# Order of the u/gate loop of a two-layer decoder trunk: both quarters of a product ahead of the reads of either, and weight sums, splits and loads in another order

## The chip, the cores and the metric

The kernel runs on one core of a Trainium2 chip. The metric is the device time of one launch in microseconds, as the median of three runs. A profile, taken in a separate execution of the same program, gives the span from its first to its last instruction and the times of the single instructions.

## The reference

A prompt of 1024 tokens and 64 sample tokens (8 sequences of 8) with 1024 features pass through two layers, all in fp32. Layer 0 is gated linear attention with four heads. Layer 1, the one that matters here, is a chunked token-mixing MLP, and a final RMSNorm follows:

```python
def cmlp_mixer(h, w_in, ln_g, ln_b, w_spatial, b_spatial, w_out):
    u, v, gate = jnp.split(h @ w_in, 3, axis=-1)
    v = layernorm(v, ln_g, ln_b)
    ...
    mixed = jnp.einsum('gts,bnsgd->bntgd', ws, vg) + bs.T[:, :, None]
    z = u * mixed.reshape(bsz, t, CMLP_WIDTH) * jax.nn.silu(gate)
    return z @ w_out, v
```

Here `h` is the RMS-normalised residual of layer 0's output, `ws` is lower triangular over chunks of 128 tokens, and u, v and gate are each 1024 features wide.

## The kernel before, in words

Features lie on the 128 partitions, in eight blocks, and 1088 token columns (1024 of the prompt, 64 of the sample) on the free axis. To keep fp32 precision each operand is split into a high part (a rounded copy that ScalarE makes) and a low part (the difference, which VectorE makes), and each product is made of three TensorE passes: high by high, high by low, low by high.

The program has five stages: the attention layer; its output projection; the v columns of layer 1 (blocks 16 to 19); the u/gate loop (`for m in range(KT)`, lines 1123 to 1233); and the last output projection with the final norm (`out_proj(28, ...)`). The change is in the u/gate loop and in the last v block, which prepares its first weights.

**The u/gate loop.** A pass m makes 128 features of u and 128 of the gate for all tokens, multiplies them with the mixed v, and stores the result z to DRAM. The product of the [u, gate] weight block (1024 by 256) with the activations is not made directly: it is cut into 2 by 2 blocks in the manner of Strassen and Winograd, which needs seven block products instead of eight. Along the inner dimension the halves are the even and the odd feature blocks, along the outer one u and gate, and the tokens form two halves of 544 columns. Each half is cut into two quarters of 272 columns (`QUART`), since a PSUM bank holds 512 fp32 numbers. So each of the seven products is made for r = 0 and r = 1, 12 matmuls each (`product`, lines 995 to 999). Its weights are four plain blocks, (1,1), (1,2), (2,1), (2,2), of which three are used as they are, and four sums and differences, s1 to s4.

The weights of pass m + 1 are made during pass m. `Quarters(blk)` loads four tiles of 256 KB into the single buffer `rawq` (lines 956 to 960, on SP's queue). `sums` makes s1 to s4 on GpSimd (line 977): s1 first, s2 from s1, s3 by itself, s4 from s2. `parts` and `plain` split a sum or a plain block into its high part on ScalarE (line 964) and its low part on VectorE (line 965); this is called a part below. The buffer `rawq` is free for the next loads when all that reads it is done, the last being the part (1,2).

The results in PSUM: `pb` (tag misc, two buffers) takes the products s2, then s1 and s4 added to it; `pa` (named p1, tag mm) takes (1,1) and later (1,2); `two` is one tile of two banks (tag sc4, one buffer), with quarter r in bank r. It takes s3 first, which ScalarE copies to the gate tile `sg` (line 1145), and later (2,2), which VectorE reads (line 1195). The dependences are tracked for the tile as a whole: where a read of quarter 0 is written ahead of the product for quarter 1, TensorE waits for that read.

Other steps of a pass: ScalarE normalises v (`v_norm`, line 1081, nine chunks of `vm`); GpSimd makes the sample rows of v for output (`v_out`, lines 1089 and 1090, with their gain and bias `bc`) and SP stores them; TensorE mixes v over the tokens (`mixed`, line 1104, and 1098 for the sample), and VectorE writes the result to `zt` (lines 1105 and 1099); GpSimd adds the copied (1,1) product to `p6` (tile half, line 1161) and `sg` (1162); VectorE reads `pb` a last time (1176); GpSimd multiplies it onto `zt` (1177, 1179); then `sg` is multiplied by the tokens' scale `rs`, goes through SiLU on ScalarE (1197) and is multiplied by `rs` again (1206 on GpSimd, 1207 on VectorE); VectorE multiplies `pa` onto `zt` (1210) and `sg` onto `zt` (1211), and SP stores `zt` to `z_d` (1212). `zt`, `sg` and `vm` have one buffer each.

**What sets the order.** From block 16 to the end of the loop the program is under `in_order()`: each engine executes its instructions in the order in which the code writes them. SP's queue, too, issues DMAs in that order, so a DMA that waits holds up all behind it. In pass 0 the four sums of the next block and its parts come at other places than later (`first`); in pass 7 there is no next block, and the loop loads and splits the weights of block 28 and the z of the first token piece instead.

Of the kernel before, what the change touches and what calls it, by code (L numbers as in the profile page):

```python
# [11 lines left out]
ALU = mybir.AluOpType  # L12
# [28 lines left out]
def trunk_kernel(ctx: ExitStack, tc: tile.TileContext, a: dict):  # L41
# [963 lines left out]
    for blk in range(16, 20):  # L1005
        cs = slice((blk - 16) * 256, (blk - 15) * 256)
        for j, i in enumerate((4, 5, 6, 7, 8, 0, 1, 2, 3) if blk == 19 else range(9)):
# [24 lines left out]
            if (blk, j) == (18, 5):  # L1032
                nxt = Quarters(20)
            if blk == 19:
                for f, at in ((t1_load, (1, 2, 5, 6)), (t1_sum, (3, 4, 7, 8)), (t1_split, (5, 6, 8, None))):
                    if j in at:
                        f(at.index(j))
                if j in (1, 2, 3):
                    nxt.sums(("s1", "s2", "s3")[j - 1])
                if j in (3, 4, 5, 6):  # L1040
                    if j == 5:
                        nxt.sums("s4")
                    if j == 6:
                        nxt.plain((1, 1))
                    else:
                        nxt.parts(("s1", "s2", "s3")[j - 3])
                V.bn_aggr(mv[:stats[i].shape[0], i, :], stats[i])
    t1_split(3)
    pr = ps("misc", "pr")
# [73 lines left out]
    for m in range(KT):  # L1123
# [10 lines left out]
        for r in R:  # L1134
            product(pb[r], w["s2"], tq[1][r])
            A.activation(p6[r], pb[r], AF.Copy)
            if first:
                cur.parts("s4") if r == 0 else cur.plain((2, 2))
        V.scalar_tensor_tensor(bias, rsum[:, g, :], lnb[:, m:m + 1], bs[:, g, :], ALU.mult, ALU.add)
        if more and not first:  # L1140
            for key in ("s1", "s2", "s3", "s4"):
                nxt.sums(key, up if key == "s4" else None)
        for r in R:
            product(pe[r], w["s3"], tq[2][r])
            A.activation(sg[:, qb[r]], pe[r], AF.Copy)
            if first and r == 0:
                cur.plain((1, 2))
                nxt = Quarters(21)
        v_norm(vm)
        v_out(m, vm, bc)  # L1150
# [3 lines left out]
        if more and not first:  # L1154
            nxt.parts("s2")
# [9 lines left out]
        V.tensor_tensor(sg[:, fb], sg[:, fb], rs_all[:, fb], ALU.mult)  # L1165
        if more and not first:
            nxt.parts("s3")
            nxt.parts("s1")
        if not more:

            zs = [act_all[:, :, :, lo:lo + n] for lo, n in zip((T - N, 0, N), size)]
            for kt in (0, 2, 4, 6):
                split(zs[0], kt, stage[:, kt, :] if kt < 5 else rest[kt - 5])
        for r in R:
            product(pb[r], w["s4"], b22[r], start=False)
            V.tensor_tensor(p1[r], p1[r], pb[r], ALU.add)
            G.tensor_tensor(zt[:, qb[r]], zt[:, qb[r]], p1[r], ALU.mult) if r == 0 else None
        mixed(zt, vm, g, m, bias, 0, True)
        G.tensor_tensor(zt[:, qb[1]], zt[:, qb[1]], p1[1], ALU.mult)
        if more:  # L1180
            vm = v_load(m + 1)
            if first:
                for key in ("s1", "s2", "s3", "s4"):
                    nxt.sums(key, up if key == "s4" else None)
            else:
                nxt.plain((1, 1))
                nxt.parts("s4")
        else:
            for kt in (1, 3, 5):
                split(zs[0], kt, stage[:, kt, :] if kt < 5 else rest[kt - 5])  # L1190
            load_w(28, 1)
            load_w(28, 2)
        for r in R:
            product(pe[r], w[2, 2], tq[3][r], start=False)
            V.tensor_tensor(sg[:, qa[r]], p6[r], pe[r], ALU.add)  # L1195
        V.tensor_tensor(sg[:, fa], sg[:, fa], rs_all[:, fa], ALU.mult)  # L1196
        A.activation(sg, sg, AF.Silu)  # L1197
        if first:
            for key in ("s2", "s3", "s1"):
                nxt.parts(key)  # L1200
        elif more:
            nxt.plain((2, 2))
        else:
            fetch_w(28, [0, 1])
            load_w(28, 3)
        G.tensor_tensor(sg[:, fb], sg[:, fb], rs_all[:, fb], ALU.mult)
        V.tensor_tensor(sg[:, fa], sg[:, fa], rs_all[:, fa], ALU.mult)
        for r in R:
            product(pa[r], w[1, 2], b21[r], start=False)
            V.tensor_tensor(zt[:, qa[r]], pa[r], zt[:, qa[r]], ALU.mult)  # L1210
        V.tensor_tensor(zt, zt, sg, ALU.mult)
        SP.dma_start(z_d[:, m, :], zt)
        if more:
            if first:
                nxt.plain((1, 1))
                nxt.parts("s4")
                nxt.plain((2, 2))
            nxt.plain((1, 2))
            if m + 2 < KT:
                following = Quarters(22 + m)  # L1220
            else:
                stage = mp.tile([P, 5, N], F32, tag="rawq", name="zstage")
                SP.dma_start(stage, z_d[:, 0:5, 0:N])
                rest = [wp.tile([P, N], F32, tag="raw", bufs=3, name="zmore") for _ in range(2)]
# [3 lines left out]
                following = None  # L1228
            cur, nxt = nxt, following
        else:  # L1230
            for p in range(2):
                split(zs[p], 7, zt[:, N * p:N * p + N])
            fetch_w(28, [2, 3])
# [142 lines left out]
```

## Time and profile before

| what | value |
|---|---|
| three runs | 1013.59, 1009.72, 1012.81 us; median 1012.81 |
| profiled execution, its own time | 1014.11 us |
| its span (first to last instruction) | 1012.3 us |
| mean granted TensorE clock | 0.966 |
| u/gate loop, first matmul of `pb` to first matmul of the last stage | 642.14 to 901.30 us |
| wait of TensorE for the reads of `two` on VectorE (line 1195) | 39.9 us in 8 waits |
| wait of GpSimd's sums for the loads of `rawq` | 65.6 us |

A row of a group says: line, engine, operation, output and inputs by tile name, shape, count; then busy time in all and mean duration of one; then the idle time of the engine just before, and what ended it. PE is TensorE's matmul, PEld its weight load, DVE VectorE, ACT ScalarE, POOL GpSimd, SPq SyncE's issuing of DMAs. A row of a timeline says: start, duration, instruction, count, and in brackets the idle time before it. A row of windows says: the stretch, its length, busy time and count of PE, PEld, DVE, ACT and POOL, then the granted share of TensorE's clock, the DMA engines' busy share, and GB/s. The chain of waits is followed back from the last instruction: at each step to what released it.

### The profile page before, as it was taken

Reading aid. Unit: us, or ns where it says so; the run is one execution under the profiler, and the core shown is the slowest. Engines: PE = TensorE matmul, PEld = TensorE weight load, DVE = VectorE, ACT = ScalarE, POOL = GpSimd, SP = SyncE. Lnnn points to the kernel's source line nnn. Section 1 sums busy time; section 2 is a strip of 40 time slices with the busy share of each in tenths; the row PEclk is TensorE's granted clock in tenths of the full one; section 3 lists DMA queues with packets and bytes.
Section 4 is the critical chain, followed back from the end, with each engine's and each line's share of the span. In section 5 each row is a group of like instructions: output and inputs, shape, how many; then the busy total and the mean of one; then the engine's idle time right before and its main releaser. Section 6 shows DMA issues by size and latency. Waiting matters only on the chain.

```text
span 1012.3 us, 17078 instructions
## 1 busy us (share of the span) xinstructions
PE 927.9 (92%) x6437; PEld 897.3 (89%) x6437; DVE 624.5 (62%) x1279; ACT 461.6 (46%) x972; POOL 283.6 (28%) x315
## 2 busy tenths in 40 slices
PE   8989999999999999899999999888797778879995
PEld 7979899989999999889999998877797778879995
DVE  7797887587758776785357555553444544484245
ACT  8673555255535554642454554633342234345332
POOL 2032242233223322221411002044432544211123
PEclk9999999999999999899999999989988889899998
DMA  8302112221231124246734445411212022355233
GB/s 279 85 3 75 58 58 69 89 58 50 76 89 58 38 84 110 65 126 188 238 99 135 149 134 174 134 52 63 91 67 90 24 90 90 107 189 148 61 102 124
DMA packets 89967, 101.80 MB, mean 101 GB/s; under 512 B 9862, under 2 KB 80844, under 8 KB 89884
## 3 DMA queue, kind: packets, MB, share of 16 engines
q1 hardware_dynamic: 89884, 100.71, 32.0%
q8 instruction: 50, 0.82, 0.3%
q14 instruction: 33, 0.27, 0.1%
HBM read 74.26 MB, written 26.42 MB: 99 GB/s over the span
## 4 chain that ended last, share of the span: by engine, by line
PE 46%; DVE 23%; DMA 9%; POOL 7%; issue 7%; ACT 6%; SPq 1%; DVEq 0%; POOLq 0%; ACTq 0%
PE fm L137 23%; PE tm L151 10%; DVE wq L965 4%; PE two L999 3%; DMA rawq<-w 3%; DMA xsum<-x_spill 2%; POOL qsum L977 2%; DVE act L198 1%; PE sc L513 1%; POOL qs L977 1%; POOL half L1161 1%; POOL sg L1162 1%; PE o L623 1%; DVE scT L526 1%; DMA xt<-x_spill 1%
## 5 line engine op out<-in xcount | busy, mean ns | idle before, releaser
L137 PE MATMUL fm<-act,w 128*128 128x384 f32 (+1 forms) x2208 | 390.6, 333 | 3.7 <-DVE zt L1210 2.5
L137 PEld LDWEIGHTS fm<-act,w 128*128 128x128 f32 x2208 | 367.6, 189 | 7.9 <-issue 2.7
L151 PE MATMUL tm<-w,act 128*128 128x256 f32 (+1 forms) x1536 | 193.5, 283 | 3.2 <-ACT vt L1010 2.2
L151 PEld LDWEIGHTS tm<-w,act 128*128 128x128 f32 x1536 | 185.6, 188 | 5.5 <-ACT vt L1010 3.1
L999 PE MATMUL two<-tsum,wq 128*128 128x272 f32 x384 | 65.8, 329 | 43.8 <-DVE sg L1195 39.9
L999 PEld LDWEIGHTS two<-tsum,wq 128*128 128x128 f32 x384 | 59.5, 223 | 47.3 <-DVE sg L1195 41.6
L123 DVE TENSOR_TENSOR w<-wr,w 128x512 fp32r<-128x512 f32 (+1 forms) x96 | 68.9, 732 | 22.6 <-ACT w L122 21.8
L122 ACT ACTIVATE w<-wr 128x512 fp32r<-128x512 f32 (+1 forms) x96 | 58.5, 624 | 28.5 <-DMA wr<-w 16.2
L821 POOL TENSOR_TENSOR acc<-acc,sq 128x384 f32<-128x384 f32 (+1 forms) x30 | 30.1, 1008 | 111.2 <-ACT sq L816 110.9
L999 PE MATMUL p<-act,wq 128*128 128x272 f32 x384 | 55.1, 303 | 0.0
L843 DVE TENSOR_TENSOR x<-fm,res 128x384 f32<-128x384 f32 (+1 forms) x40 | 20.9, 526 | 54.4 <-PE fm L137 54.4
L999 PEld LDWEIGHTS p<-act,wq 128*128 128x128 f32 x384 | 54.2, 205 | 0.0
L999 PE MATMUL pb<-act,wq 128*128 128x272 f32 x384 | 51.4, 290 | 0.0
L816 ACT ACTIVATE sq<-x 128x384 f32<-128x384 f32 (+1 forms) x42 | 20.9, 503 | 61.8 <-DVE x L843 59.6
L999 PEld LDWEIGHTS pb<-act,wq 128*128 128x128 f32 x384 | 49.0, 189 | 0.0
L1197 ACT ACTIVATE sg<-sg 128x1088 f32<-128x1088 f32 x8 | 8.9, 1114 | 84.8 <-DVE sg L1196 84.8
L468 POOL TENSOR_TENSOR xe<-xe,k 128x384 f32<-128x384 f32 (+2 forms) x24 | 29.1, 1213 | 44.3 <-ACT xe L467 41.1
L654 POOL TENSOR_TENSOR on<-on,g 128x384 f32<-128x384 f32 (+1 forms) x24 | 23.8, 1013 | 57.4 <-DVE on L653 34.7
L977 POOL TENSOR_TENSOR qsum<-rawq 128x512 f32<-128x512 f32 x16 | 20.7, 1296 | 65.7 <-DMA rawq<-w 65.6
L444 POOL TENSOR_TENSOR kd<-kd,k 128x384 f32<-128x384 f32 (+1 forms) x12 | 12.0, 1003 | 84.5 <-ACT kd L443 84.5
L965 DVE TENSOR_TENSOR wq<-qsum,wq 128x512 fp32r<-128x512 f32 x25 | 19.6, 810 | 26.0 <-ACT wq L964 26.0
L475 DVE TENSOR_TENSOR xl<-cum 128x192 f32<-128x192 f32 (+4 forms) x72 | 35.0, 511 | 0.0
(260 smaller groups left out, 1580.6 us busy)
## 6 DMA issues: line engine op xcount, KB each, us to landing
wr<-w SPq DMA_DIRECT2D x92, 256.0 KB, 3.1
rawq<-w SPq DMA_DIRECT2D x32, 256.0 KB, 4.5
xsum<-x_spill SPq DMA_DIRECT2D x16, 272.0 KB, 3.1
z_spill<-zt SPq DMA_DIRECT2D x8, 544.0 KB, 3.0
s<-s SPq DMA_DIRECT2D x16, 256.0 KB, 4.2
state_s<-ns SPq DMA_DIRECT2D x32, 128.0 KB, 1.8
v_spill<-vt SPq DMA_DIRECT2D x32, 128.0 KB, 3.0
vm<-v_spill SPq DMA_DIRECT2D x8, 512.0 KB, 4.2
```

Of the source, the lines that this page charges most:

```text
L122: A.activation(w[:, 0], raw, AF.Copy)
L123: V.tensor_tensor(w[:, 1], raw, w[:, 0].bitcast(F32), ALU.subtract)
L137: PE.matmul(acc, lhs, rhs, start=(k == 0), stop=(k == 23))
L151: PE.matmul(acc, lhs, rhs, start=(k == 0), stop=(k == 23))
L468: G.tensor_tensor(xe, xe, kt_[:, :nl], ALU.mult)
L475: V.tensor_tensor(l3[:, :, lo:hi], c3[:, :, (i + 1) * m:], r, ALU.subtract)
L654: G.tensor_tensor(o, o, gate[h][:, j, t0:t0 + n], ALU.mult)
L816: A.activation(sq, raw[p][:, m, :], AF.Square)
L821: (V if gain is not None and p == 2 or m == KT - 1 else G).tensor_tensor(total, acc[p], sq, ALU.add)
L965: V.tensor_tensor(w[:, 1], src, w[:, 0].bitcast(F32), ALU.subtract)
L977: G.tensor_tensor(t, x, y, op)
L999: PE.matmul(acc, lhs, rhs, start=start and k + i == 0, stop=k + i == 5, skip_group_check=not start)
```

## The change

Three things change, and no arithmetic on TensorE.

First, at both uses of `two` the products of both quarters are now written ahead of the reads of either: s3 ahead of ScalarE's copies, and (2,2) ahead of VectorE's reads.

Second, the preparation of the next weights is in one order for all passes. The sums s1 and s2 stand ahead of GpSimd's adds to `half` and `sg`, s3 behind them, and s4 behind `v_out`, which moves from the normalisation to behind the two products onto `zt`. The parts s2, s3, s1 stand ahead of the reads of `two`, then (1,1), (2,2) and (1,2); s4's part moves to the start of the pass that uses it. The next loads of `rawq` follow the part (1,2) directly, ahead of the reads of `pa` and the store of z, which is now issued behind these loads. Four of the nine normalisations of v move ahead of ScalarE's copies of `two` in passes 1 to 7. The product of `rs` and half of `sg` after SiLU moves from GpSimd to VectorE.

Third, at the edges: the first loads of `rawq` are called two steps later in v block 18, the first sums and parts in block 19 lie one step later, the tile `pr` moves from tag misc to tag o, and in pass 7 weight loads and splits are spread otherwise, with the last product onto `zt` in two pieces.

```diff
-            if (blk, j) == (18, 5):
+            if (blk, j) == (18, 7):
                 nxt = Quarters(20)
...
-    pr = ps("misc", "pr")
+    pr = ps("o", "pr")
...
         for r in R:
             product(pb[r], w["s2"], tq[1][r])
             A.activation(p6[r], pb[r], AF.Copy)
-            if first:
-                cur.parts("s4") if r == 0 else cur.plain((2, 2))
+        cur.parts("s4")
+        if first:
+            for key in ((1, 2), (2, 2)):
+                cur.plain(key)
+            nxt = Quarters(21)
...
-        if more and not first:
-            for key in ("s1", "s2", "s3", "s4"):
-                nxt.sums(key, up if key == "s4" else None)
         for r in R:
             product(pe[r], w["s3"], tq[2][r])
+        if not first:
+            v_norm(vm, range(4))
+        for r in R:
             A.activation(sg[:, qb[r]], pe[r], AF.Copy)
...
-        v_norm(vm)
-        v_out(m, vm, bc)
+        v_norm(vm, range(0 if first else 4, 9))
...
-        if more and not first:
-            nxt.parts("s2")
+        if more:
+            for key in ("s1", "s2"):
+                nxt.sums(key)
...
-        V.tensor_tensor(sg[:, fb], sg[:, fb], rs_all[:, fb], ALU.mult)
-        if more and not first:
-            nxt.parts("s3")
-            nxt.parts("s1")
-        if not more:
+        if more:
+            nxt.sums("s3")
+        else:
...
         G.tensor_tensor(zt[:, qb[1]], zt[:, qb[1]], p1[1], ALU.mult)
+        v_out(m, vm, bc)
         if more:
+            nxt.sums("s4", up)
             vm = v_load(m + 1)
...
+        V.tensor_tensor(sg[:, fb], sg[:, fb], rs_all[:, fb], ALU.mult)
+        if more:
+            for key in ("s2", "s3", "s1"):
+                nxt.parts(key)
...
         for r in R:
             product(pe[r], w[2, 2], tq[3][r], start=False)
+        for r in R:
             V.tensor_tensor(sg[:, qa[r]], p6[r], pe[r], ALU.add)
+        if more:
+            nxt.plain((1, 1))
...
-        G.tensor_tensor(sg[:, fb], sg[:, fb], rs_all[:, fb], ALU.mult)
         V.tensor_tensor(sg[:, fa], sg[:, fa], rs_all[:, fa], ALU.mult)
-        for r in R:
-            product(pa[r], w[1, 2], b21[r], start=False)
-            V.tensor_tensor(zt[:, qa[r]], pa[r], zt[:, qa[r]], ALU.mult)
-        V.tensor_tensor(zt, zt, sg, ALU.mult)
-        SP.dma_start(z_d[:, m, :], zt)
+        V.tensor_tensor(sg[:, fb], sg[:, fb], rs_all[:, fb], ALU.mult)
         if more:
...
             nxt.plain((1, 2))
             if m + 2 < KT:
                 following = Quarters(22 + m)
...
+        for r in R:
+            product(pa[r], w[1, 2], b21[r], start=False)
+            V.tensor_tensor(zt[:, qa[r]], pa[r], zt[:, qa[r]], ALU.mult)
+        for part in ((slice(0, T),) if more else (slice(0, N), slice(N, T))):
+            V.tensor_tensor(zt[:, part], zt[:, part], sg[:, part], ALU.mult)
...
+        SP.dma_start(z_d[:, m, :], zt)
```

Lines of the changed kernel are some three to six lower or higher than before: the reads of `two` are at 1194, the adds to `half` and `sg` at 1158 and 1159, the last product onto `zt` at 1217.

On TensorE, in a later pass (any of 2 to 6), from the sample's mixing to the product (1,2) in `pa`; the tile names are those of the code, `tsum` are the activation's sums, and brackets name the engines whose semaphore a matmul waits for. Before:

```order
L1098 MATMUL mix<-wss,vm 128x64 [waits DVE_49,Activation_49,Pool_49]
L999 MATMUL two<-tsum_6114,wq 128x272 x12
L999 MATMUL two<-tsum_6114,wq 128x272 [waits DVE_49]
L999 MATMUL two<-tsum_6114,wq 128x272 x11
L999 MATMUL p_8380<-act,wq 128x272 [waits Activation_49]
L999 MATMUL p_8380<-act,wq 128x272 x11
```

After:

```order
L1095 MATMUL mix<-wss,vm 128x64 [waits DVE_49,Activation_49,Pool_49]
L999 MATMUL two<-tsum_6114,wq 128x272 x24
L999 MATMUL p_8370<-act,wq 128x272 [waits Activation_49]
L999 MATMUL p_8370<-act,wq 128x272 x11
L999 MATMUL p_8371<-act,wq 128x272 [waits Activation_49]
```

The 24 matmuls of both quarters of (2,2) now follow each other without a wait between them; before, the thirteenth waited for VectorE.

On GpSimd in one such pass (`half` is p6 and the copied (1,1) product, `qsum` are s1, s2, s3 and `qs4` is s4). Before, from the first sum:

```order
L977 TENSOR_TENSOR qsum_8030<-rawq_7986 128x512
L977 TENSOR_TENSOR qsum_8032<-qsum_8030,rawq_7986 128x512
L977 TENSOR_TENSOR qsum_8034<-rawq_7986 128x512
L977 TENSOR_TENSOR qs4_8036<-rawq_7986,qsum_8032 128x512
L1089 TENSOR_TENSOR bc_7994<-vm_7912,bc_7994 64x128
L1090 TENSOR_TENSOR bc_7994<-bc_7994 64x128
L1161 TENSOR_TENSOR half_7999<-half_7999,half_8001 128x272
L1162 TENSOR_TENSOR sg_7993<-sg_7993,half_8001 128x272
L1161 TENSOR_TENSOR half_8000<-half_8000,half_8002 128x272
L1162 TENSOR_TENSOR sg_7993<-sg_7993,half_8002 128x272
L1177 TENSOR_TENSOR zt_7992<-zt_7992,half_8001 128x272
L1179 TENSOR_TENSOR zt_7992<-zt_7992,half_8002 128x272
```

After, from the first sum:

```order
L977 TENSOR_TENSOR qsum_8366<-rawq_8230 128x512
L977 TENSOR_TENSOR qsum_8368<-qsum_8366,rawq_8230 128x512
L1158 TENSOR_TENSOR half_8271<-half_8271,half_8273 128x272
L1159 TENSOR_TENSOR sg_8265<-sg_8265,half_8273 128x272
L1158 TENSOR_TENSOR half_8272<-half_8272,half_8274 128x272
L1159 TENSOR_TENSOR sg_8265<-sg_8265,half_8274 128x272
L977 TENSOR_TENSOR qsum_8414<-rawq_8230 128x512
L1176 TENSOR_TENSOR zt_8264<-zt_8264,half_8273 128x272
L1178 TENSOR_TENSOR zt_8264<-zt_8264,half_8274 128x272
L1086 TENSOR_TENSOR bc_8266<-vm_8177,bc_8266 64x128
L1087 TENSOR_TENSOR bc_8266<-bc_8266 64x128
L977 TENSOR_TENSOR qs4_8450<-rawq_8230,qsum_8368 128x512
```

The four sums and the two operations on `bc` stood ahead of the adds to `half` and `sg`; now two sums do, and s3, `bc` and s4 stand behind.

On VectorE, the end of such a pass (`wq<-qsum` is the part of a sum, `wq<-rawq` of a plain block, `wq<-qs` of s4). Before, from the last reads of `pb`:

```order
L1176 TENSOR_TENSOR half<-half,pb 128x272 x2
L1099 SCALAR_TENSOR_TENSOR zt<-mix,lng,bias 128x64
L965 TENSOR_TENSOR wq<-rawq,wq 128x512
L965 TENSOR_TENSOR wq<-qs_8586,wq 128x512
L1195 TENSOR_TENSOR sg<-half,two 128x272 x2
L1196 TENSOR_TENSOR sg<-sg,rs 128x544
L965 TENSOR_TENSOR wq<-rawq,wq 128x512
L1207 TENSOR_TENSOR sg<-sg,rs 128x544
L1210 TENSOR_TENSOR zt<-p_8655,zt 128x272
L1210 TENSOR_TENSOR zt<-p_8656,zt 128x272
L1211 TENSOR_TENSOR zt<-zt,sg 128x1088
L965 TENSOR_TENSOR wq<-rawq,wq 128x512
```

After, from the parts of the sums, which follow the last reads of `pb`, the sample's mixing and a product with `rs`:

```order
L965 TENSOR_TENSOR wq<-qsum,wq 128x512 x3
L1194 TENSOR_TENSOR sg<-half,two 128x272 x2
L965 TENSOR_TENSOR wq<-rawq,wq 128x512
L1197 TENSOR_TENSOR sg<-sg,rs 128x544
L965 TENSOR_TENSOR wq<-rawq,wq 128x512
L1203 TENSOR_TENSOR sg<-sg,rs 128x544
L1204 TENSOR_TENSOR sg<-sg,rs 128x544
L965 TENSOR_TENSOR wq<-rawq,wq 128x512
L1215 TENSOR_TENSOR zt<-p_8370,zt 128x272
L1215 TENSOR_TENSOR zt<-p_8371,zt 128x272
L1217 TENSOR_TENSOR zt<-zt,sg 128x1088
L965 TENSOR_TENSOR wq<-qs_8450,wq 128x512
```

The last row of `wq<-rawq`, which frees the buffer for the next loads, stood behind the last product onto `zt`; now it stands ahead of the reads of `pa`. The reads of `two` now stand next to each other with one part less ahead of them, and s4's part ends the pass.

On SP's queue the four loads of `rawq` followed the store of z in each pass, and the store now follows them; the loads of the next `vm`, behind the store of the v rows in both, now wait for the later operations on `bc`.

More of the change, by code (lines that the diff above doesn't have):

```diff
@@ L1037, in trunk_kernel @@
                         f(at.index(j))
[L1038 to L1046, printed above, removed]
+                if j in (2, 3, 4, 6):
+                    nxt.sums({2: "s1", 3: "s2", 4: "s3", 6: "s4"}[j])
+                if j in (4, 5, 6):
+                    nxt.parts(("s1", "s2", "s3")[j - 4])
+                if j == 7:
+                    nxt.plain((1, 1))
                 V.bn_aggr(mv[:stats[i].shape[0], i, :], stats[i])
     t1_split(3)
-    pr = ps("misc", "pr")
+    pr = ps("o", "pr")
     PE.matmul(pr, ones, ws.rearrange("p g t -> p (g t)"), start=True, stop=True)
@@ L1176, in trunk_kernel @@
             V.tensor_tensor(p1[r], p1[r], pb[r], ALU.add)
-            G.tensor_tensor(zt[:, qb[r]], zt[:, qb[r]], p1[r], ALU.mult) if r == 0 else None
+            if r == 0:
+                G.tensor_tensor(zt[:, qb[r]], zt[:, qb[r]], p1[r], ALU.mult)
         mixed(zt, vm, g, m, bias, 0, True)
         G.tensor_tensor(zt[:, qb[1]], zt[:, qb[1]], p1[1], ALU.mult)
+        v_out(m, vm, bc)
         if more:
+            nxt.sums("s4", up)
             vm = v_load(m + 1)
[L1182 to L1187, printed above, removed]
+        V.tensor_tensor(sg[:, fb], sg[:, fb], rs_all[:, fb], ALU.mult)
+        if more:
+            for key in ("s2", "s3", "s1"):
+                nxt.parts(key)
         else:
@@ L1190, in trunk_kernel @@
                 split(zs[0], kt, stage[:, kt, :] if kt < 5 else rest[kt - 5])
-            load_w(28, 1)
-            load_w(28, 2)
+            load_w(28, 3)
         for r in R:
             product(pe[r], w[2, 2], tq[3][r], start=False)
+        for r in R:
             V.tensor_tensor(sg[:, qa[r]], p6[r], pe[r], ALU.add)
+        if more:
+            nxt.plain((1, 1))
         V.tensor_tensor(sg[:, fa], sg[:, fa], rs_all[:, fa], ALU.mult)
         A.activation(sg, sg, AF.Silu)
[L1198 to L1201, printed above, removed]
+        if more:
             nxt.plain((2, 2))
         else:
-            fetch_w(28, [0, 1])
-            load_w(28, 3)
-        G.tensor_tensor(sg[:, fb], sg[:, fb], rs_all[:, fb], ALU.mult)
+            fetch_w(28, [1, 2])
         V.tensor_tensor(sg[:, fa], sg[:, fa], rs_all[:, fa], ALU.mult)
-        for r in R:
-            product(pa[r], w[1, 2], b21[r], start=False)
-            V.tensor_tensor(zt[:, qa[r]], pa[r], zt[:, qa[r]], ALU.mult)
-        V.tensor_tensor(zt, zt, sg, ALU.mult)
-        SP.dma_start(z_d[:, m, :], zt)
+        V.tensor_tensor(sg[:, fb], sg[:, fb], rs_all[:, fb], ALU.mult)
         if more:
[L1214 to L1217, printed above, removed]
             nxt.plain((1, 2))
@@ L1223, in trunk_kernel @@
                 SP.dma_start(stage, z_d[:, 0:5, 0:N])
+                following = None
+        for r in R:
[3 more added lines that the diff above has]
+            V.tensor_tensor(zt[:, part], zt[:, part], sg[:, part], ALU.mult)
+            if not more:
+                k = int(part.start > 0)
+                split(zs[k], 7, zt[:, N * k:N * k + N])
+        SP.dma_start(z_d[:, m, :], zt)
+        if more:
+            if m + 2 == KT:
                 rest = [wp.tile([P, N], F32, tag="raw", bufs=3, name="zmore") for _ in range(2)]
@@ L1227, in trunk_kernel @@
                 load_w(28, 0)
[L1228 removed]
             cur, nxt = nxt, following
         else:
[L1231 to L1233 removed]
+            fetch_w(28, [3])
     order.close()
```

6 lines of the change are left out of this document (3 added, 3 removed).

## Prediction

> **What bounds the kernel now.** I read the page first: span and TensorE's share of it.
>
> ```profile
> span 1012.3 us, 17078 instructions
> PE 927.9 (92%) x6437; PEld 897.3 (89%) x6437; DVE 624.5 (62%) x1279; ACT 461.6 (46%) x972; POOL 283.6 (28%) x315
> ```
>
> TensorE is the busy engine, but 92% is a mean over stages. Then the groups by line, for the line that the change is about, and the windows of one pass of the u/gate loop, of a stretch after its long wait, and of the stage behind the loop.
>
> ```profile
> L999 PE MATMUL two<-tsum,wq 128*128 128x272 f32 x384 | 65.8, 329 | 43.8 <-DVE sg L1195 39.9
> 734.90:767.20 32.30, 25.68 (x187) 25.25 (x187) 14.62 (x23) 10.72 (x23) 12.76 (x14) 0.87 0.22 71
> 767.20:770.20 3.00, 3.00 (x13) 3.00 (x14) 0.00 (x0) 0.00 (x0) 0.00 (x0) 0.50 0.00 0
> 910.20:1012.30 102.10, 90.55 (x536) 88.64 (x536) 45.02 (x74) 36.78 (x69) 23.28 (x21) 0.97 0.35 111
> ```
>
> TensorE waits 39.9 us in all for VectorE's reads of the first quarter of `two` (L1195), and after such a wait runs some 3 us at a granted clock of 0.50. What is a pass worth to TensorE alone? The timeline of TensorE in one pass:
>
> ```profile
> 751.35 3.18 PE L999 MATMUL p<-act,wq 128*128 128x272 f32 x24
> 754.37 1.95 PE L1104 MATMUL mix<-ws,vm 128*128 128x128 f32 x16
> 756.07 3.26 PE L999 MATMUL pb<-act,wq 128*128 128x272 f32 x24
> 767.19 1.05 PE L999 MATMUL two<-tsum,wq 128*128 128x272 f32 x3 [6.13 <-DVE sg L1195]
> ```
>
> A pair of quarters takes 3.02 us from start to start (751.35 to 754.37), the mixing 1.70 (754.37 to 756.07). Seven pairs (21.14), the mixing and 0.11 for the sample's mixing (an estimate: eight mixings of 128 columns take 1.70, this one has 64) make 22.95 us. A pass takes 32.3. So 9.3 us of each pass are waits and slow clock, more than the 5 us that the waits for L1195 sum to per pass. Why is VectorE late? The chain of waits through the same pass:
>
> ```profile
> 743.93 1.29 DVE zt L1211
> 745.22 0.60 DVE wq L965
> 746.24 0.72 SPq L959
> ...
> 747.53 4.75 DMA rawq<-w
> ...
> 752.51 1.29 POOL qsum L977
> ...
> 753.88 1.34 POOL qsum L977 x2
> ...
> 756.35 1.75 POOL qs L977
> ...
> 759.00 0.76 POOL half L1161
> ...
> 761.22 0.72 POOL sg L1162
> ...
> 762.61 1.29 DVE wq L965 x2
> 763.89 0.69 DVE half L1176 x2
> ...
> 764.78 2.00 DVE wq L965 x2
> 766.78 0.36 DVE sg L1195
> ...
> 767.19 3.10 PE two L999 x12
> ...
> 770.79 0.74 DVE sg L1196
> ...
> 773.27 1.50 DVE wq L965
> 774.77 0.64 DVE sg L1207
> ...
> 776.21 1.29 DVE zt L1211
> 777.50 0.60 DVE wq L965
> ```
>
> This is a ring, and it sets the period: L1211 starts at 743.93 and 776.21, 32.28 us apart. The one buffer `rawq` is free when VectorE has made the last part of its block (L965 at 745.22); then come the loads, all four sums on GpSimd, the bias rows, the half/sg adds, VectorE's parts and L1195, the second quarter on TensorE, and the tail of the pass down to the next last part. TensorE's long wait is one link of it.
>
> **The change, part by part.** The new ring is put together from the same rows. (a) Loads: the z store is now issued behind them. From the last part's end (745.82) to the first sum (752.51) is 6.69 us today with the store ahead; without it, one issue 0.72, the data 4.75 and 0.22 of hand-over make 5.69. Bounds 5.2 and 6.7; I take 5.7. (b) Only s1 and s2 stand ahead of the half/sg adds: 753.88 less 752.51 is 1.37, and 1.29 more, 2.66; today all four sums and the bias rows stand there (752.51 to 759.00, 6.49). (c) The four adds, 759.00 to 761.94, stay: 2.94. (d) Second read of pb 0.35, sample's mixing 0.20, the product with rs 0.64, together 1.2. (e) Three parts, 1.29 for two, so 1.93. (f) Both reads of `two`, 0.36 each, which now follow each other, 0.72; TensorE's 3.10 between them leaves the ring. (g) Part (1,1) 0.64 and the product with rs 0.74. (h) From that product's end (771.53) over SiLU and ScalarE's copy to the next part (773.27) 1.74. (i) Part (2,2), two products with rs and part (1,2): 2.52. The reads of pa and L1211 (2.09 today, 775.41 to 777.50) leave the ring, since part (1,2) now goes ahead of them. Sum: 5.69 + 2.66 + 2.94 + 1.2 + 1.93 + 0.72 + 1.38 + 1.74 + 2.52 = 20.8.
>
> To this comes what GpSimd and VectorE do to each other. Timelines of both engines:
>
> ```profile
> 740.57 1.37 POOL L1206 TENSOR_TENSOR sg<-sg,rs 128x544 f32<-128x544 f32 x1 [6.37 <-ACT sg L1197]
> 740.98 1.51 DVE L965 TENSOR_TENSOR wq<-rawq,wq 128x512 fp32r<-128x512 f32 x1 [1.76 <-ACT wq L964]
> ```
>
> The part that takes 0.60 alone takes 1.51 beside L1206 and ends 0.55 after it. This meeting goes (L1206 moves to VectorE, +0.64 there, counted in i). But s3, the two zt products, the bias rows and s4 now run on GpSimd just while VectorE makes d, e and g: two sums of 1.29 and four pieces of at most 0.76, 5.6 us in all. The cost is 0 if they never meet, 5.6 if VectorE stands still through all of them. In the row above the part lost 0.91 of the 1.37 it met; at that rate all pieces would cost 3.7. I take that somewhat over half of them are met, 2.15 (0.45 for the product in d, 1.0 for the parts e, 0.7 behind s4). The ring is then 22.95 (20.8 to 26.4).
>
> The Trainium skill (page "SBUF — State Buffer", section "SBUF: two separate sides") has a rule that speaks against this order: a VectorE operation with two SBUF inputs and a GpSimd operation that reads SBUF lock each other out for the whole instruction. By the rule at its worst the ring would be 26.4 and the kernel about 972; without any lock it would be 20.8, and TensorE's 22.95 the bound. The trace agrees that there is a lock (1.51 against 0.60); how often they meet in the new order, no row shows.
>
> So ring and TensorE (both 22.95) are even, and two that are even don't mesh without loss: I forecast 23.4 us a pass, an estimate that allows 0.45 for hand-overs. To the count of passes and the two ends:
>
> ```profile
> L1211 DVE TENSOR_TENSOR zt<-zt,sg x8: 1279/1292/1295, 677.9 to 901.9; 128x1088 f32<-128x1088 f32 x8
> 872.54 1.30 DVE zt L1211
> 873.86 3.13 DMA z_spill<-zt
> ...
> 878.01 4.33 DMA bc<-lnbc
> ...
> 883.45 0.66 POOL half L1161
> 901.30 1.98 PE L137 MATMUL fm<-act,w 128*128 128x384 f32 x10 [2.48 <-DVE zt L1210]
> 646.53 2.45 PE L999 MATMUL pb<-tsum,wq 128*128 128x272 f32 x12 [2.32 <-ACT rsum L1051]
> ```
>
> Six passes from the first L1211 to the seventh take 872.54 - 677.9 = 194.6 us, 32.4 each; at 23.4 they take 140.4, which is 54.2 less. The last pass, from the seventh L1211's end (873.84) to the next stage's first product (901.30), takes 27.46. Of this, 9.6 pass before the half adds (store, 4.33 for the bias rows behind other loads, two small operations). In the new order those adds don't stand behind the bias rows and can start when ScalarE's copy is there, about 3 us in; 6.6 are gained there, and the second quarter's wait goes as well, which I put at 0.9, since the splits of `zmore` behind it still wait for the z store. I take 7.5 less (5 to 9). At the start, `pr` in its own buffer takes away the 2.32 us wait; VectorE's and ScalarE's weights stand right behind it, so I count 1.0 (0 to 2.3). Moving the first block's loads from step 5 to 7 and its sums by one step lies beside the v products on TensorE; I count nothing, and were that cover gone, one load time of 6.7 at the worst. Given back: the last stage was fed by loads that have no more time than before, and its products start 7.5 us nearer to them; 1.5 (0 to 4). Sum: 54.2 + 7.5 + 1.0 - 1.5 = 61.2 us.
>
> The profiled execution took 1014.11 us, 1.8 more than its span; the median of the three runs is 1012.81. 1012.81 - 61.2 = 951.6, rounded to 952.
>
> **The rivals.** (1) A longer ring: the loads stay at 6.7 and VectorE and GpSimd stand in each other's way twice as much (4.3). The ring is then 22.95 + 1.0 + 2.15, and 0.4 for hand-overs, 26.5; the six passes give 35, and the time is about 970. For it: the pieces do lie beside each other. Against: the z store's data no longer stand ahead of the loads. This is the rule of the Trainium skill's page "SBUF — State Buffer" named above, taken near its worst. (2) The z store, now behind 1 MB of loads, holds the single zt buffer: the first mixing result (L1105 before, L1102 now) waits for it, and TensorE's sample product stands behind that. L1217 ends 2.1 after the last part, when 3.4 of the loads' 5.5 us are left, and the store alone takes 3.13: landing at most 6.5 after L1217, the result 0.7 later. TensorE needs the first of the parts e at about 11.5 after L1217 for its next pass and has two pairs (6.04) to do between, so it comes to the sample product at 5.5 or later. The wait is at most 1.7 us a pass; at 1.5 the time is 961. For it: there is one buffer only. Against: the store's data may overlap the loads'. (3) Slower than before: ScalarE now normalises four chunks of v ahead of its copies of `two`, and their load stands in SP's queue behind v_out, which waits for the bias rows, now late on GpSimd.
>
> ```profile
> DMA to landing us min/median/max: 3.7/4.0/4.2
> ```
>
> That is the load of vm. The first sum starts 3.6 after L1217 (5.7 less 2.1); b, c, s3 and 3.5 for the zt and bias pieces bring the issue to 14 and the landing to 18. The four normalisations stand 3 us ahead of the copies of `two`, which wait for the next L1217 at 23.4, so the load is wanted at about 20. Each us beyond that adds up to one to every pass; the kernel is slower than before from a landing some 9 us late, after 29. Nothing in the trace holds this load that long. (4) No change: the ring is tied to something the trace does not show, and keeps 32.3. Against it: links (a), (b) and (f) are explicit in the chain and are cut in the new order.
>
> **How the numbers follow.** My forecast, with (2) as its upper part, 0.80; rival 1, 0.13; rival 4, 0.03; rival 3, 0.04. The forecast's own bounds: TensorE's floor of 22.95 in all passes (57), 9 at the end and 2.3 at the start, nothing given back, make 68 and 944; 24.9 a pass, (2)'s price, make 52 and 961. Rival 1 reaches to 970, a bit of it beyond. So 944 to 972. A measurement of this kernel tells about 0.5% from no change, 5 us: faster by more 0.93, within 0.03, slower 0.04.
>
> **What would show it.** In the changed profile L1217 starts every 23 to 24 us; the group two<-tsum loses its wait for the reads of `two` and its mean comes down from 329 ns towards 290; the granted clock in the loop is above 0.95; the first sum starts 5.5 to 6 us after the last part; the chain of waits in the loop names TensorE's products for a good part. I am wrong if TensorE waits over 2 us a pass anywhere (then by whom: L1102 for rival 2, weights for rival 1, L1145 for rival 3), if the period is over 26, or if the stage behind the loop takes over 115 us against 111.0 today (901.30 to 1012.3).

## The result and the profile after

The changed kernel takes 952.25 us (median of 4 runs, 951.49 to 953.75) beside 1011.26 (4 runs, 1007.81 to 1013.59): 0.942 of the time, with a 95% interval of 0.939 to 0.945. The forecast was 952. The profiled execution took 951.55 with a span of 949.8.

First the page's head and two of TensorE's groups by line (the prediction shows the head and the group `two` of before):

```profile
span 949.8 us, 17088 instructions
PE 909.2 (96%) x6437; PEld 882.1 (93%) x6437; DVE 630.6 (66%) x1288; ACT 458.8 (48%) x972; POOL 279.8 (29%) x307
L999 PE MATMUL pb<-act,wq 128*128 128x272 f32 x384 | 52.1, 292 | 5.3 <-ACT half L1133 5.2
L999 PE MATMUL two<-tsum,wq 128*128 128x272 f32 x384 | 51.6, 290 | 0.0
```

The products into `two` wait for nothing now (43.8 us before) and take 290 ns each (329). What TensorE still waits for in the loop is 5.2 us in all, for ScalarE's copy of pb (L1133). A window of one pass, from 0.33 us behind the end of one L1217 (744.37) to as much behind the end of the next, shows the granted clock (its last columns are clock, share and rate of the DMA engines):

```profile
744.70:768.19 23.49, 23.38 (x188) 23.16 (x188) 15.74 (x25) 10.25 (x24) 12.23 (x13) 1.00 0.30 95
```

TensorE is busy for 23.4 of these 23.5 us at a clock of 1.00 (0.87 in the pass of before). It would be easy to read this as "TensorE sets the pass". The chain of waits from the first sum in this pass to the first sum of the next says otherwise:

```profile
748.13 1.28 POOL qsum L977
...
750.74 0.77 POOL half L1158
...
752.96 0.74 POOL sg L1159
...
754.36 1.15 DVE sg L1183
755.51 0.71 DVE wq L965
...
756.62 2.12 DVE wq L965 x2
758.74 0.69 DVE sg L1194 x2
759.43 1.43 DVE wq L965
760.87 0.65 DVE sg L1197
...
762.55 0.62 ACT wq L964
...
763.20 0.69 DVE wq L965
763.89 0.63 DVE sg L1203
764.53 0.64 DVE sg L1204
765.16 0.61 DVE wq L965
...
767.17 4.66 DMA rawq<-w
...
772.00 1.28 POOL qsum L977
```

There is no product in it. It is the ring through the buffer `rawq`, sum to sum 23.87 us here. The first seven L1217 end at 670.73, 695.27, 719.72, 744.37, 767.86, 791.72 and 816.39: 24.28 a pass on average, against 32.44 before.

Where the 62.5 us between the two profiled spans went, by stage (landmarks: the first `tm` product of the v stage, the first product of the loop, the ends of the first and seventh zt*sg, the first `fm` product, the end):

| stretch | before | after | difference | forecast |
|---|---|---|---|---|
| up to the v stage | 539.15 | 536.49 | -2.7 | 0 |
| v stage | 102.99 | 100.19 | -2.8 | 0 |
| first pass | 37.03 | 34.05 | -3.0 | -1.0 |
| six passes | 194.67 | 145.66 | -49.0 | -54.2 |
| last pass | 27.46 | 20.54 | -6.9 | -7.5 |
| last stage | 111.0 | 112.87 | +1.9 | +1.5 |

The code ahead of the v stage is the same in both kernels; its start lies between 535.3 and 538.2 in the profiles of all the experiments, so the 2.7 there belongs to no edit. The profiled execution of before took 1014.11, longer than the median of 1011.26: so the spans differ by 62.5 and the medians by 59.0.

### The profile page after: what moved, and what is told of

Same layout as the page of the kernel before. It is cut to its first block, busy times and chain, and to the rows that moved or that the text cites. A ratio compares the mean times of both kernels' runs of the same rounds, so it can differ in the third digit from the quotient of the medians.

```text
span 949.8 us, 17088 instructions
## 1 busy us (share of the span) xinstructions
PE 909.2 (96%) x6437; PEld 882.1 (93%) x6437; DVE 630.6 (66%) x1288; ACT 458.8 (48%) x972; POOL 279.8 (29%) x307
## 3 DMA queue, kind: packets, MB, share of 16 engines
q1 hardware_dynamic: 89884, 100.71, 34.1%
## 4 chain that ended last, share of the span: by engine, by line
PE 46%; DVE 24%; DMA 11%; issue 6%; ACT 6%; POOL 5%; SPq 2%; DVEq 0%; POOLq 0%; ACTq 0%
PE fm L137 26%; PE tm L151 10%; DVE wq L965 4%; DMA rawq<-w 3%; DMA xsum<-x_spill 3%; DMA wr<-w 1%; PE sc L513 1%; POOL qsum L977 1%; PE o L623 1%; PE pst L584 1%; SPq L959 1%; POOL half L1158 1%; DVE sg L1183 1%; DMA xt<-x_spill 1%; DVE scT L526 1%
## 5 line engine op out<-in xcount | busy, mean ns | idle before, releaser
L999 PE MATMUL two<-tsum,wq 128*128 128x272 f32 x384 | 51.6, 290 | 0.0
L999 PE MATMUL p<-act,wq 128*128 128x272 f32 x384 | 51.0, 288 | 0.0
L999 PEld LDWEIGHTS p<-act,wq 128*128 128x128 f32 x384 | 49.4, 188 | 0.0
L999 PEld LDWEIGHTS two<-tsum,wq 128*128 128x128 f32 x384 | 49.1, 188 | 0.0
L964 ACT ACTIVATE wq<-qsum 128x512 fp32r<-128x512 f32 x25 | 15.0, 626 | 52.3 <-POOL qsum L977 52.3
L1102 DVE SCALAR_TENSOR_TENSOR zt<-mix,lng,bias 128x512 f32<-128x512 f32 x16 | 11.4, 747 | 31.9 <-DMA z_spill<-zt 21.3
```

Source lines behind the costliest of these rows:

```text
L999: PE.matmul(acc, lhs, rhs, start=start and k + i == 0, stop=k + i == 5, skip_group_check=not start)
```

## The experiments

Two theories were set against each other. **Ring theory** (the prediction's; a ring is a chain of waits that closes on itself from one pass to the next): the loop through the one buffer `rawq` (loads, sums, adds, parts) sets the pass, and the pair edit only takes one link out of it. **Pair theory**: the pair edit removes TensorE's waits and slow clock, 9 us a pass, and the order of sums, parts and loads is worth little. Ratios and differences are to the kernel before on the same chip in the same session (medians 1012.38 for the first four, 1012.23 for the next four, 1011.52 for the last three). "Pass" is the mean of the six passes in the profile.

| kernel | us | ratio, 95% interval | pass |
|---|---|---|---|
| pair edit alone | 984.58 | 0.973 (0.970 to 0.975) | 28.68 |
| order alone (all of the change but the pair edit) | 1000.0 | 0.987 (0.984 to 0.990) | 30.74 |
| loads behind the store | 969.67 | 0.958 (0.955 to 0.961) | 27.14 |
| parts and loads early | 945.84 | 0.935 (0.932 to 0.937) | 22.98 |
| store after the loads | 946.71 | 0.935 (0.932 to 0.938) | 23.45 |
| s1 twice | 962.93 | 0.950 (0.946 to 0.954) | 25.55 |
| early, s1 twice | 946.37 | 0.935 (0.932 to 0.938) | 23.23 |
| edges as before | 954.55 | 0.944 (0.940 to 0.947) | 24.33 |
| rs on GpSimd | 951.4 | 0.939 (0.936 to 0.942) | 24.37 |
| order alone, s1 twice | 999.94 | 0.988 (0.985 to 0.991) | 30.61 |
| early, and late store | 946.27 | 0.935 (0.933 to 0.938) | 23.49 |

**The pair edit alone**, in the kernel before (the same at the second use of `two`):

```diff
         for r in R:
             product(pe[r], w["s3"], tq[2][r])
+        for r in R:
             A.activation(sg[:, qb[r]], pe[r], AF.Copy)
```

> The kernel before, with one edit: at both uses of `two` both quarters' products stand ahead of both reads. Ring theory (the loop through the one buffer rawq sets the pass; the pair edit cuts one link of it): the link is the second quarter's 3.10 us on TensorE and some 0.3 of hand-over, 3.4 a pass; the sums, bias rows and loads stay, so L1211 comes every 28.9 us (32.3 less 3.4), seven passes of gain make 24 and the last 1 to 3: about 985 us (980 to 991). Pair theory (TensorE's waits for the reads of `two` and the half clock behind them, 9.3 us a pass, are the loss, and the pair edit takes them away whatever the order of the weights): a pass of 23.5, about 950 to 958.

It took 984.58 with passes of 28.68, where the ring theory had 985 and 28.9. TensorE no longer waits for the reads of `two`, but for something else; its waits, and two lines of the chain in a pass:

```profile
PE mix L1098 <- DVE zt L1105: 17.7, 5, 4.4
```

```profile
762.98 4.39 DMA rawq<-w
...
774.00 0.75 POOL half L1162
```

The wait has moved to the sample's mixing, where TensorE arrives early and stands behind VectorE's mixing (L1105, at 771.89 in this pass). This stands behind the part of s2, whose high part on ScalarE (L964) waits for GpSimd's sums and so for the loads. VectorE's timeline:

```profile
770.89 1.08 DVE L965 TENSOR_TENSOR wq<-qsum,wq 128x512 fp32r<-128x512 f32 x1 [7.92 <-ACT wq L964]
```

What comes later in the ring waits for GpSimd's adds, and these start 6.6 us after the loads' data (767.37), because all sums and the bias rows stand ahead. As a whole explanation the pair theory falls here.

**The order alone**, the reads put back between the quarters:

```diff
-        for r in R:
-            product(pe[r], w["s3"], tq[2][r])
         if not first:
             v_norm(vm, range(4))
         for r in R:
+            product(pe[r], w["s3"], tq[2][r])
             A.activation(sg[:, qb[r]], pe[r], AF.Copy)
 ...
         for r in R:
             product(pe[r], w[2, 2], tq[3][r], start=False)
-        for r in R:
             V.tensor_tensor(sg[:, qa[r]], p6[r], pe[r], ALU.add)
```

> The kernel after, with the reads of `two` put back between the two quarters at both uses (the first four normalisations then stand ahead of the products); the new order of sums, parts and loads stays. Ring theory: the second quarter's products (3.1) come back into the ring of 24.3, with 0.2 to 0.4 of hand-over: 27.6 a pass, six passes 20 and the last pass 3 more: about 974 (966 to 982). The gains of this kernel (some 38 over the kernel before) and of the pair edit alone (some 27) then add up to that of the whole change (59). Pair theory: the waits of 6 us are back and the order of the weights is worth little: 995 to 1010.

It took 1000.0, which the ring theory missed by 26 and the pair theory had. The chain of waits through a pass shows why:

```profile
770.48 0.29 ACT sg L1144
...
770.82 1.78 PE two L999 x12
772.59 3.00 PE pb L999 x24
775.60 3.03 PE p L999 x24
778.63 1.78 PE mix L1101 x16
780.41 3.02 PE pb L999 x24
...
783.55 0.44 DVE half L1173
...
784.19 0.63 DVE sg L1182
784.82 4.11 DVE wq L965 x3
788.93 0.36 DVE sg L1192
...
789.33 2.39 PE two L999 x12
791.72 3.93 PE p L999 x24
```

This is a second ring that has neither loads nor sums in it. TensorE's products feed VectorE (L1173); behind that stand the product with rs and three parts; the read of the first quarter (L1192) stands behind these; and TensorE's second quarter, and so all its later products, waits 4.18 us for that read and 1.32 for ScalarE's copy. With the slow products after the wait (2.2 a pass: the groups p and two take 57.6 and 62.7 us in all, against 51.0 and 51.6) and TensorE's own 22.95 it makes 30.6. I had counted the interleaving as one link of 3.1 in the first ring; it closes a ring of its own. So the theory is amended: **two rings**, one through `rawq` and one through TensorE and the reads of `two`, and the longer one sets the pass.

**The second ring, put to a test**: s1 made twice in this kernel, which lengthens only the ring through `rawq`.

```diff
-            for key in ("s1", "s2"):
+            for key in ("s1", "s1", "s2"):
                 nxt.sums(key)
```

> The kernel with the new order but the reads of `two` between the quarters (1000.0 us), with the sum s1 made twice. Its chain of waits runs through TensorE, ScalarE and VectorE and not through the loads and sums. If that second ring sets its pass (30.6), the 1.29 more on GpSimd is inside the idle time ahead of the half/sg adds (1.2) and costs 0 to 0.3 a pass: 999 to 1003. If the ring through rawq sets it, 1.29 on each of seven passes: 1009.

999.94 against 1000.0, passes of 30.61: it cost nothing, as the two rings have it. (Before the adds GpSimd stands idle for 1.21 us in a pass of the kernel above, so nearly all of the 1.29 had room there. No run lengthens the second ring by itself: that it sets this pass rests on its chain and on this test.)

**The same dose in the changed kernel** (the same edit):

> The kernel after, with the sum s1 of each block made twice (one more GpSimd operation of 1.29 us ahead of the half/sg adds, with the same result). Ring theory: GpSimd's sums stand in the ring, so each of the seven passes grows by 1.29: 9 us, 961 (959 to 963). If the pass were TensorE's (23.1 of 24.3), no more than a part of it would show: 952 to 955.

962.93: 10.7 more than the changed kernel by the medians of two sessions, 8 by the ratios. In the profile the pass grew by 1.27 to 25.55, which is 7.7 over six passes, and the first pass by 2.1. Although TensorE is busy for 23.4 us of a pass, GpSimd's 1.29 passes straight into the time. In one pass the chain of waits names the z store ahead of s2 (6.14 us, then L1102, which ends at 760.32). But s2 starts at 760.34, 0.08 after the second s1, as it does after s1 in the changed kernel, so the store holds nothing up there.

**Loads behind the store again:**

```diff
-            if m + 2 < KT:
-                following = Quarters(22 + m)
 ...
         SP.dma_start(z_d[:, m, :], zt)
         if more:
+            if m + 2 < KT:
+                following = Quarters(22 + m)
```

> The kernel after, with the next block's loads issued behind the z store again. The store waits for L1217, which ends 2.1 us after the last part, so the loads start 2.1 to 2.5 later. Ring theory: the pass grows by that, less what the loads gain by having fewer of the store's packets at their end (0 to 1): 25.8 to 26.8 a pass, 9 to 15 more over six passes: 961 to 967. Pair theory: TensorE sets the pass and 0.5 to 1.3 a pass is slack: 952 to 955, and no growth of the period beyond 0.5.

969.67, more than the 961 to 967 that I had put down: the loads are issued 0.55 after L1217's end instead of 2.02 ahead of it, 2.57 later, the first sum comes 2.9 later, and the pass takes 2.86 more. The delay goes through one to one; what I had allowed the loads to get back, they didn't get. (In pass 6 the load of z for the next stage, which follows the same lines, moves with them.)

**The store after the loads**, on ScalarE's queue in the next pass (for passes 0 to 5):

```diff
-        zt = up.tile([P, T], F32, tag="zt", name="zt")
 ...
             A.activation(p1[r], pa[r], AF.Copy)
+        if 0 < m < KT - 1:
+            A.dma_start(z_d[:, m - 1, :], zt)
+        zt = up.tile([P, T], F32, tag="zt", name="zt")
 ...
-        SP.dma_start(z_d[:, m, :], zt)
+        if m + 2 >= KT:
+            SP.dma_start(z_d[:, m, :], zt)
```

> The kernel after, with the z store of passes 0 to 5 issued on ScalarE's queue in the next pass, behind the two copies of p1, some 2.7 to 3.3 us after L1217 and so near the end of the rawq loads instead of at their start; zt is allocated again behind it. Theory A (the loads stayed at 6.7 us because the store's packets share the engines with them): without it the first sum comes 1.0 earlier, as step (a) of the forecast had it; the pass falls from 24.3 to 23.3, which is near TensorE's 23.1: 945 to 948. Theory B (the loads take that long by themselves): no gain there, and the first mixing result now waits up to 0.6 longer for zt: 951 to 956.

946.71. The table of DMA issues (the last number is the median us from issue to landing), first of the changed kernel, then of this one:

```profile
rawq<-w SPq DMA_DIRECT2D x32, 256.0 KB, 3.8
...
z_spill<-zt SPq DMA_DIRECT2D x8, 544.0 KB, 6.0
```

```profile
rawq<-w SPq DMA_DIRECT2D x32, 256.0 KB, 3.2
...
z_spill<-zt ACTq DMA_DIRECT2D x6, 544.0 KB, 2.7
```

In the changed kernel the store is issued 0.7 us behind the last of the four loads. The medians of the loads (3.8 and 3.2) rest on the ten landings that each profile shows, and they don't tell: the kernels with s1 twice and with rs on GpSimd issue in the order of the changed kernel, and their median is 3.2 too. The store's figure is one landing in each profile: 4.6 to 6.0 in the six kernels with the store 0.7 behind the loads, 2.7 or 2.8 in the four where it is issued later.

What tells is the time from the last part's end to the first sum. It is 5.9 to 7.0 in the changed kernel (mean of six passes 6.63) and 5.3 to 6.3 here (5.81; step (a) of the forecast had 5.69). In the five other kernels with the store 0.7 behind the loads the means are 6.45 to 6.69. In the three others with the store later, all of them with the early loads that come next, they are 5.59 to 5.89, and in two of these (5.59 and 5.61) the store stays on SP's queue and is issued some 6 us behind the first load. So the shared queue alone doesn't cost the time; the store being under way beside the loads does. (No run issues the store at its old time on another queue.) Relative to L1217's end the first sum comes 0.83 earlier here, and the pass is 0.83 shorter.

**Parts and loads early**, straight behind the parts s2, s3, s1 (the same lines go out of their places further down):

```diff
         for r in R:
             product(pe[r], w[2, 2], tq[3][r], start=False)
+        if more:
+            for key in ((1, 1), (2, 2), (1, 2)):
+                nxt.plain(key)
+            if m + 2 < KT:
+                following = Quarters(22 + m)
 ...
         for r in R:
             V.tensor_tensor(sg[:, qa[r]], p6[r], pe[r], ALU.add)
 ...
```

> The kernel after, with the parts (1,1), (2,2), (1,2) and the next loads put straight behind the three parts s2, s3, s1, ahead of the reads of `two`, the products with rs and the SiLU. Ring theory: these (0.72, 0.65, 1.74, 1.28) leave the ring of 24.3, which comes down to 19.9; TensorE's 22.95 is then the bound, a pass of 23.0 to 23.5, 5 to 8 us less over six passes: 944 to 947. If the pass is TensorE's already (pair theory), nothing changes: 951 to 954. If instead the reads of `two` and the SiLU, now later, hold up L1217 and with it the next pass's first products, it is slower: 955 to 960.

945.84, and now the chain of waits through a pass is of TensorE alone:

```profile
740.90 1.36 PE pb L999 x11
742.26 3.03 PE p L999 x24
745.29 1.78 PE mix L1101 x16
747.08 3.01 PE pb L999 x24
750.09 0.17 PE mix L1095 x2
750.25 3.07 PE two L999 x24
753.33 3.02 PE p L999 x24
756.35 3.01 PE pb L999 x24
759.36 3.01 PE two L999 x24
762.37 2.63 PE pb L999 x21
```

Five passes in a row take 23.11 to 23.12: that is TensorE's floor (the prediction had put it at 22.95). This kernel is faster than the changed one; its interval (0.932 to 0.937) lies below that of the changed kernel (0.939 to 0.945).

**What hides behind that floor.** s1 twice in this kernel (the edit shown above), and the early loads together with the late store (both edits as above):

> The same second s1 in the kernel with the early parts and loads (945.8 us, whose passes of 23.1 are TensorE's). Ring theory: its ring is 19.9 and has 3.2 to spare, so 1.29 more costs nothing: 944 to 948 (period 23.1 as without it). If a ring through GpSimd still sets the pass there: 953 to 955.

> The kernel with early parts and loads (945.8) and with the late z store (946.7 by itself) at once. The passes of the first are TensorE's already (23.11), so the two gains do not add: 943 to 948. If they did add: about 940.

946.37 and 946.27, against 945.84. Where the ring is shorter than TensorE's floor the second s1 costs nothing: from the third pass on, passes take 23.10 to 23.12 with it and without it. Only in the first two, before this holds, the profile with s1 twice is 3.8 longer. And the 5 us of the late store aren't there twice. In the profile with both edits some passes are even longer than the floor: one takes TensorE 24.2, because the late store holds `zt`, VectorE's L1102 waits 5.95 for it, and TensorE's sample product waits for L1102:

```profile
PE mix L1095 <- DVE zt L1102: 0.9, 1, 0.9
```

**The edits outside the loop undone** (first block's loads, sums and parts, and pr):

```diff
-            if (blk, j) == (18, 7):
+            if (blk, j) == (18, 5):
 ...
-    pr = ps("o", "pr")
+    pr = ps("misc", "pr")
```

> The kernel after, with the edits outside the loop undone: the first block's loads at step 5 of block 18, its sums and parts a step earlier in block 19, pr in a misc buffer. The forecast counted 1.0 for pr (0 to 2.3) and nothing for the loads and sums: 952 to 954. The profiles before and after differ by 2.8 in the v stage and 3.0 up to the first L1217; if the edits are the cause: 956 to 958. If these differences are between runs: 951 to 952.

954.55: 2.3 more by the medians, though the intervals overlap (0.940 to 0.947 and 0.939 to 0.945). The profiles settle part of it. In the three with the old edges the v stage takes 102.99, 104.68 and 104.20; in the ten others 99.5 to 102.0. The cause shows in VectorE's timeline, and behind it TensorE's, of this kernel:

```profile
616.44 1.50 DVE L932 TENSOR_TENSOR xsum<-xsum 128x272 f32<-128x272 f32 x1 [4.51 <-POOL xsum L931]
617.98 1.41 DVE L933 TENSOR_TENSOR xsum<-xsum 128x272 f32<-128x272 f32 x1
619.42 1.40 DVE L934 TENSOR_TENSOR xsum<-xsum 128x272 f32<-128x272 f32 x1
```

```profile
621.61 2.81 PE L151 MATMUL tm<-w,act 128*128 128x256 f32 x12 [1.87 <-ACT vt L1010]
```

and in VectorE's timeline of the changed kernel:

```profile
617.12 0.44 DVE L932 TENSOR_TENSOR xsum<-xsum 128x272 f32<-128x272 f32 x1 [4.23 <-POOL xsum L931]
617.59 0.44 DVE L933 TENSOR_TENSOR xsum<-xsum 128x272 f32<-128x272 f32 x1
618.07 0.44 DVE L934 TENSOR_TENSOR xsum<-xsum 128x272 f32<-128x272 f32 x1
```

With the sums a step earlier, GpSimd makes three of them (616.37 to 620.52) just while VectorE splits the x sums: each of these ends 0.3 us behind the end of a sum, and the next v products wait 1.87 us. A step later, the sums start at 619.98, after all three. The wait for `pr` is back too, at 1.1 us, but the first pass, in which it lies, is no longer for it (33.4 against 34.1).

**The product with rs back on GpSimd:**

```diff
-        V.tensor_tensor(sg[:, fb], sg[:, fb], rs_all[:, fb], ALU.mult)
+        G.tensor_tensor(sg[:, fb], sg[:, fb], rs_all[:, fb], ALU.mult)
```

> The kernel after, with the product of rs and sg[fb] behind the SiLU back on GpSimd. If GpSimd and VectorE hold each other up as they did in the kernel before (a part took 1.51 beside this product, 0.60 without), VectorE saves 0.64 in the ring and loses 0.9 on what it does beside it: 0.3 a pass more, 952 to 956. If they don't, the ring loses 0.64 a pass: 947 to 949.

951.4, and 24.37 a pass against 24.28. The part (2,2) beside it, in VectorE's timeline:

```profile
765.20 1.47 DVE L965 TENSOR_TENSOR wq<-rawq,wq 128x512 fp32r<-128x512 f32 x1 [1.70 <-ACT wq L964]
```

It took 0.69 in the changed kernel (763.20 in the chain above), so VectorE loses 0.8 and saves 0.64. As to the time this is no difference that can be told: moving this product, which the prediction counted at about even, shows no gain here.

## Why the prediction was right, point by point

**The total is right, and partly by compensation.** The six passes gave 49.0 instead of 54.2. In the profiles, what was missing came from places where less or nothing was counted: 2.0 more in the first pass, 2.8 in the v stage, 2.7 ahead of it that is no edit's. By the medians the whole gain is 59.0 instead of 61.2, from a base that lies 1.55 below the 1012.81 of the forecast, since a fourth run came in. That all this cancelled to within 1 us is luck; that the six passes gave most of the gain is not.

**The ring, step by step**, from the chain shown above (b to i; a as the mean of six passes):

| step | forecast | measured |
|---|---|---|
| a: loads | 5.69 | 6.63 |
| b: s1, s2 | 2.66 | 2.61 |
| c: four adds | 2.94 | 2.96 |
| d: read of pb, sample, rs (with 0.45 for GpSimd) | 1.65 | 1.81 |
| e: three parts (with 1.0) | 2.93 | 3.23 |
| f: reads of `two` | 0.72 | 0.69 |
| g: part (1,1), rs (with 0.7) | 2.08 | 2.09 |
| h: SiLU, copy | 1.74 | 1.68 |
| i: (2,2), two rs, (1,2) | 2.52 | 2.57 |
| sum | 22.93 | 24.27 |

The mechanism was right and one term was mis-sized: **step (a)**. It took the z store's data to be out of the loads' way once the store was issued behind them. Issued 0.7 us behind, it still holds them up: the step is 0.9 longer than forecast. Issued late it gives 5.81 and takes 0.83 off the pass, and with the loads early step (a) is 5.59, so this is shown and not only argued. The Trainium skill (page "DMA: Bandwidth & Descriptors", section "Two DMAs through the same engine are not ordered") says that descriptors of one queue start in order but are pipelined, so that order of issue is not order of completion. No run here shows in which order they completed; the runs agree in that being first in the queue didn't give the loads the time that they have with the store out of the way.

The rest of the miss is 0.45 for GpSimd's and VectorE's meetings, put at 2.15 and measured at 2.6 (0.6 in d, 1.3 in e, 0.7 in g). The forecast's 23.4 thus held an allowance for two even chains that fell to one chain being 1.2 longer than the other.

**What was expected to show.** Right: `two` lost its wait and takes 290 ns, the clock is 1.00, TensorE waits at most 1.2 us a pass, the last stage takes 112.9. Wrong: the first sum comes 6.6 after the last part instead of 5.5 to 6, the period is 23.5 to 24.7 instead of 23 to 24, and the chain in the loop names no product at all.

**The share of the pair edit** ("TensorE's long wait is one link of it") was too small a view, though it didn't touch the sum, since the forecast was for both edits at once. Alone the pair edit takes 27.8 us off, the order 12.4, both together 59.0. The 18.8 that only both together give is the sign of two rings: cut one, and the other still holds the pass (28.7 or 30.7).

**The ends.** The last pass (7.5 against 6.9) and the last stage (1.5 against 1.9) were right. `pr` was counted at 1.0; the wait that its own buffer removes is 1.1 with the old edges and 2.3 in the kernel before, but no run shows that the first pass is shorter without it. The first pass gave 3.0. The two kernels with the reads between the quarters and single sums take 37.0 and 40.2 for it, those with the pair edit and single sums 33.1 to 34.3. So the pair edit, which I had counted only from the first L1217 on, is the likely cause here too. The size is not shown: with s1 twice it is 37.1 without the pair edit, and 36.1 and 35.8 with it. The v stage was counted at nothing, with the v products named as cover; the cover had a hole, VectorE's splits, which feed these products.

**The rivals.** (1) The longer ring came half true: 24.3, between 23.4 and 26.5, its first half (loads at 6.7) nearly in full, its second (4.3 for the meetings) not. (2) The wait for zt exists: L1102 waits 21.3 us for the z store in five waits. In the changed kernel it costs nothing: VectorE has to wait 1.5 us for GpSimd's adds right behind it (744.37 to 767.86), and TensorE's list of waits has no L1102. In the late-store kernel it is longer (27.1 in six) and that kernel is faster; TensorE waits behind it in two profiles, once in each: 0.6 with the old edges, 0.9 with the early loads and the late store. (3) TensorE has no wait for L1145 in its list of waits, so the load of vm is in time. (4) fell with the result.

## What to carry to other kernels

Look for all closed rings through a wait before pricing its removal: one edit alone gains only down to the next ring, and the gains of two edits neither add up nor can be read by subtraction. An engine that is busy for 95% of a pass or more need not be what sets it; a dose (one operation twice) on the other chain tells, with 1.27 us a pass in one kernel and nothing in the later passes of the other here. And a store issued just behind a load is not out of its way, although the load stands first in the queue: put it where the load has landed, or issue the load earlier.

## What the runs showed of the hardware that I had not expected

A 544 KB store issued 0.7 us behind the last of four loads of 256 KB on the same queue lengthened the time from the last part's end to the first sum from 5.6 to 5.9 us (means of four kernels) to 6.5 to 6.7 (six kernels), and itself took 4.6 to 6.0 instead of 2.7 or 2.8. On the same queue but some 6 us behind the first load it cost nothing that shows. And three VectorE operations in a row that take 0.44 us alone took 1.50, 1.41 and 1.40 beside three GpSimd sums of 1.27 to 1.47 us: each ended 0.3 us behind the end of a sum, so that 1.3 us of work took 4.4.
